# Attention on one Trainium2 core: scores, values and filler as three streams at uniform rates instead of units of two query tiles, with eight row buffers

## The chip, the cores and the metric

The kernel runs on one core of one Trainium2 chip, as one launch. The metric is the device time in microseconds (us). The kernel before was timed in three runs; the number compared is their median. A profiled execution of the same kernel was recorded beside them.

## The reference

One layer of a hybrid encoder on 1024 frames of width 1024: three token mixers beside each other, merged by sigmoid gates, then a gated MLP. What matters here are the two attentions, eight heads each, and the two other jobs that share the stage with them.

```python
hn = rms_norm(x, norm_mix_g[l])
u = hn @ w_in[l]
u_mla, u_fox, u_ssm, u_gate = jnp.split(u, split_at, axis=-1)
y_a = mla_branch(u_mla, ...) @ w_br_mla[l]
y_b = fox_branch(u_fox, ...) @ w_br_fox[l]
y_c = ssm_branch(u_ssm, ...) @ w_br_ssm[l]
g = jax.nn.sigmoid(u_gate + b_gate[l])
...
s = jnp.einsum('bqhd,bkhd->bhqk', q_blk, k).astype(jnp.float32) * scale
p = jax.nn.softmax(bias_mask(i, s), axis=-1).astype(v.dtype)
return jnp.einsum('bhqk,bkhd->bqhd', p, v)
```

MLA (the first eight heads) lets a query see all keys of its own and of earlier chunks of 64; FOX (the last eight) is causal with a decay. Both are computed row by row of 128 queries, and row i needs the keys of tiles 0 to i only.

## The kernel before

**The stage.** The kernel goes through input projections, the two attentions, the state-space scan (SSD), the merge of the branches, and the MLP. In the attention stage TensorE has three kinds of work, and the order in which it gets them is written out by hand: PE is under a manual schedule, and Python generators issue pieces of work in the order that a small planner chooses. The other engines get their instructions through a queue of due times.

**Scores** (`score_row`, L1288, through `scores`, L1332). For row i of a head, n = i + 1 key tiles: the score matmuls of one or two chunks of columns (at least 256 wide) into a PSUM buffer, three passes for an MLA head and two for a FOX head (`o.passes`). Then `finish` (L1310): for FOX one more matmul that adds the causal mask (L1313), and for both the softmax: row maximum on VectorE (L1314), exponential with row sum on ScalarE (L1316), reciprocal on VectorE and scaling on GpSimd (`norm`, L1319 to L1321). The row stands in one of the `a_pm` buffers (`Ring`, L1422), six of them. For FOX `finish` is put in the list `held`, so that the mask matmul can be placed right ahead of a group of transposes.

**Values** (`values`, L1337). For a unit jp, which is the two rows 2 jp and 2 jp + 1: transposes of the normalised rows in groups (L1379), split into a high and a low part by ScalarE (L1384) and VectorE (L1385), and the products with the values (`pv`, L1341), which run two key pairs behind the transposes (`PVLAG`, `pend`). Before its first transpose the function forces the softmax of both rows out of the queue (L1369). `done` (L1354) adds the two halves of the accumulator and stores them.

**Filler** (`all_fill`, L1163). 36 blocks of the remaining columns of the input projection (L1181), 12 with a convolution and 24 gates, in pieces of six matmuls. It is used to fill the waits of the attentions and of the SSD; whatever remains is issued after them.

**The planner.** Every generator yields the cost of what it has issued, in us of the planner's own clock `clk` (called plan-us below); `advance` (L1206) adds it to the clock, and `run_until` issues what has fallen due for the other engines. `merge` (L1222) takes a set of generators, each with its expected total, and always advances the one that has done the smallest part of its total, until all have ended.

**Units.** The loop at L1437 goes through 64 units (16 heads of four). In step n one `merge` runs together the scores of unit n, the values of unit n - 2, and filler of 1.08 times the cost of both (`FILL_ATT`, L1417; the share counts three passes for FOX too). A unit's values therefore start when the whole of the step after its scores has been issued. The costs are those of `cost_s` (L1411: columns times passes over 2400, and 0.1 per unit) and `cost_v` (L1414). With the score stream come the loads: at unit 0 of a head the queries and keys of the next head (`load_head`, L1257), at unit 3 its values (`load_values`, L1277, two buffers), all on the queue of SyncE, which also carries the filler's weights and all stores.

**After attention** the SSD stage (L1612) merges its own generators with filler of fixed amounts, and takes what filler there is.

The line that decides how far the values trail the scores:

```python
                if n >= 2:
                    share += cost_v(done[n - 2][1])
                    me = []
                    me.append(values(*done[n - 2], me))
                    tp_next[:] = me
                    st.append((me[0], cost_v(done[n - 2][1])))
                merge(st, FILL_ATT * share)
```

Of the kernel before, what the change touches and what calls it, by code (L numbers as in the profile page):

```python
# [11 lines left out]
F32 = mybir.dt.float32  # L12
# [9 lines left out]
P = 128  # L22
D = 1024
S = 1024
# [18 lines left out]
def block_kernel(ctx: ExitStack, tc: tile.TileContext, x, positions, norm_mix_g, w_in, b_gate,  # L43
# [581 lines left out]
    with ExitStack() as pm:  # L625
# [119 lines left out]
        def values():  # L745
            nonlocal step
            i = next(fxv)
            if i == NT:
                for _ in step:
                    pass  # L750
                vcols.append(v2)
            fox_values(i)
            next(step, None)
# [35 lines left out]
        units = 0  # L789
# [11 lines left out]
        for t in range(6):  # L801
# [4 lines left out]
            units = t  # L806
            fx_head.append(fx_bank())
            fx_part(fx_head[t], t, 0, 4, lambda k: w0[0][:, k, :], lambda k: w0[1][:, k, :])
        units = 0
# [25 lines left out]
    yv, yn, e, rec, s_, s2, q_, mn = (ft(n) for n in ("yv", "yn", "e", "rec", "s_", "s2", "q_", "mn"))  # L835
# [367 lines left out]
    fill = all_fill()  # L1203
    owed = [0.0]

    def advance(gen):  # L1206
        c = next(gen, None)
        if c is not None:
            clk[0] += c
            run_until(clk[0])  # L1210
        return c

    held, tp_next = [], []

    def flush():
        while held:
            held.pop(0)()
# [33 lines left out]
                s_[2] += c  # L1251


    class Head:
        pass

    def load_head(pool, br, h):  # L1257
        o = Head()
        o.br, o.h = br, h
        if (8 * br + h) % 2 == 0:  # L1260
            t = [e[:, i, :] for e in (w0p.tile([P, 2, S], F32R, name=uid(n), tag=n) for n in ("w0h", "w0l"))
                 for i in range(2)]
        else:
            t = [pool.tile([P, S], F32R, name=uid(n), tag=n, bufs=1) for n in ("qk0", "qk1", "qk2", "qk3")]
        if br == 0:
            parts = ((0, 0, k_h), (1, 0, k_l), (2, 0, q_h), (3, 0, q_l))
            kh, kl, qh, ql = (e[0:96] for e in t)
            o.passes = ((t[2][0:104], t[0][0:104]), (qh, kl), (ql, kh))
        else:
            parts = ((0, 0, fk_h), (1, 0, fk_h[:, 0:64, :]), (1, 64, fk_l), (2, 0, fq_h), (2, 64, fq_h), (3, 0, fq_l))  # L1270
            o.passes = ((t[2], t[1]), (t[3][0:68], t[0][0:68]))
        for i, r, src in parts:
            n = src.shape[1]
            SY.dma_start(f32(t[i][r:r + n, :]), src[h])
        return o

    def load_values(pool, o):  # L1277
        o.vv = pool.tile([P, NT, P], F32R, name=uid("vv"), tag="vv")
        SY.dma_start(f32(o.vv), (v_d, fv_d)[o.br].rearrange("(t p) h c -> p t h c", p=P)[:, :, o.h, :])
# [52 lines left out]
    def scores(o, jp, pn):  # L1332

        for i in (2 * jp, 2 * jp + 1):
            yield from score_row(o, i, pn)

    def values(o, jp, pn, me):  # L1337

        po = o_acc[:, jp % 2, :]

        def pv(kp, th, tl):  # L1341
            full = kp < jp
            k0, k1 = 2 * kp, 2 * kp + 1
            T.matmul(po, o.vv[:, k0, :], th[:, 0:256], start=kp == 0, stop=False)
            if full:
                T.matmul(po, o.vv[:, k1, :], th[:, 256:512], start=False, stop=False)
                T.matmul(po, o.vv[:, k1, :], tl[:, 256:512], start=False, stop=False)
            else:
                T.matmul(po[0:64, 128:256], o.vv[:, k1, 0:64], th[:, 256:384], start=False, stop=False)
                T.matmul(po[0:64, 128:256], o.vv[:, k1, 64:128], th[:, 256:384], start=False, stop=False)  # L1350
                T.matmul(po[0:64, 128:256], o.vv[:, k1, 0:64], tl[:, 256:384], start=False, stop=False)
            T.matmul(po, o.vv[:, k0, :], tl[:, 0:256], start=False, stop=not full)  # L1352

        def done():  # L1354
            o1, l1 = a_o1.get()
            o2, l2 = a_o2.get()
            later(0.5, lambda: A.activation(o1, po[64:128, :], AF.Copy))

            t_done[0] = clk[0]

            def fin():
                V.tensor_add(o2, po[0:64, :], o1)  # L1362
                SY.dma_start(att_d[o.br][o.h * 64:o.h * 64 + 64, jp * 256:jp * 256 + 256], o2)

            l1[0] = l2[0] = o_last[jp % 2] = later(0.9, fin)

        flush()
        for _, rl in pn:
            force(rl[0])  # L1369
        for k0 in range(0, jp + 1, 2):  # L1370
            flush()
            tp_next.clear()
            cs = 0.0
            for kp in range(k0, min(k0 + 2, jp + 1)):
                pt, pl = a_tp.get()
                off = 0
                for k in (2 * kp, 2 * kp + 1):
                    for qi in ((0, 1) if k <= 2 * jp else (1,)):
                        T.transpose(pt[:, off:off + P], pn[qi][0][:, k * P:k * P + P], ident)  # L1379
                        off += P  # L1380
                th, _ = a_th.get()
                tl, _ = a_tl.get()
                cs += 0.11 * off / P
                later(cs + 0.05, lambda th=th, pt=pt, off=off: A.activation(th[:, :off], pt[:, :off], AF.Copy))  # L1384
                pl[0] = later(cs + 0.6, lambda th=th, tl=tl, pt=pt, off=off: V.tensor_sub(  # L1385
                    tl[:, :off], pt[:, :off], f32(th[:, :off])))
                pend.append((pv, kp, th, tl, pl, jp, done if kp == jp else None))
            yield cs
            while len(pend) > PVLAG:
                if pend[0][1] == 0 and clk[0] - t_done[0] < 1.0:  # L1390
                    yield 0.0
                run_pv()
                if len(pend) <= PVLAG and k0 + 2 <= jp:
                    tp_next.append(me[0])
                yield 0.44

    PVLAG = 2
    pend = []
# [12 lines left out]
    def cost_s(jp, n=3):  # L1411
        return sum(n * max(b - a, 256) / 2400 for i in (2 * jp, 2 * jp + 1) for a, b in row_chunks(i)) + 0.1

    def cost_v(jp):  # L1414
        return 0.88 * jp + 0.33 + 0.39

    FILL_ATT = 1.08  # L1417
    FILL_SSD = [11.3] * 8 + [12.0, 24.5]
    with ExitStack() as pt__:
        atp = pt__.enter_context(TP("atp", 2))  # L1420
        psp = pt__.enter_context(TP("psa", 1, space=PSUM))
        a_pm = Ring(atp, [P, S], F32, "pm", 6)  # L1422
        a_nmx, a_rs = (Ring(atp, [P, 4], F32, n, 4) for n in ("nmx", "rs"))
        a_th, a_tl = (Ring(atp, [P, 512], F32R, n, PVLAG + 2) for n in ("pth", "ptl"))
        a_o1 = Ring(atp, [64, 256], F32, "o1", 1)
        a_o2 = Ring(atp, [64, 256], F32, "o2", 4)
        a_s = Ring(psp, [P, S], F32, "s", 2)
        a_tp = Ring(psp, [P, 512], F32, "tp", 2)
        o_acc = psp.tile([P, 2, 256], F32, name="o", tag="o")
        with tc.manual_schedule(engines={mybir.EngineType.PE}):  # L1430
            names = [(br, h) for br in range(2) for h in range(8)]
            merge([], 5.0)
            units = [(n, jp) for n in range(16) for jp in range(4)]
            heads = {0: load_head(atp, *names[0])}
            load_values(atp, heads[0])
            done = []
            for n in range(len(units) + 2):  # L1437
                st, share = [], 0.0
                if n < len(units):
                    hn_, jp = units[n]  # L1440
                    if jp == 0 and hn_ + 1 < 16:
                        heads[hn_ + 1] = load_head(atp, *names[hn_ + 1])
                    if jp == 3 and hn_ + 1 < 16:
                        load_values(atp, heads[hn_ + 1])
                    pn = []
                    done.append((heads[hn_], jp, pn))
                    share += cost_s(jp)
                    st.append((scores(heads[hn_], jp, pn), cost_s(jp, len(heads[hn_].passes))))
                if n >= 2:
                    share += cost_v(done[n - 2][1])  # L1450
                    me = []
                    me.append(values(*done[n - 2], me))
                    tp_next[:] = me
                    st.append((me[0], cost_v(done[n - 2][1])))
                merge(st, FILL_ATT * share)
            flush()
            while pend:
                run_pv()
                clk[0] += 0.44
                run_until(clk[0])  # L1460
            run_until(clk[0] + 3.0)
# [8 lines left out]
    with ExitStack() as ps__:  # L1470
# [141 lines left out]
        with tc.manual_schedule(engines={mybir.EngineType.PE}):  # L1612
# [6 lines left out]
            for c in range(NT + 2):  # L1619
                st = []  # L1620
# [13 lines left out]
    with ExitStack() as pe_:  # L1634
# [39 lines left out]
        for b, wsrc, nk in ((1, w_br_fox, 4), (0, w_br_mla, 4), (2, w_br_ssm, 8)):  # L1674
# [3 lines left out]
            for k in range(nk):  # L1678
# [13 lines left out]
                else:  # L1692
                    h, l = fox_hl[k] if b == 1 else ops_tile(4 + k)
                    e = split(h, l, raw)
# [8 lines left out]
            for j in range(NK):  # L1703
# [11 lines left out]
                g = fpl.tile([P, S], F32, name=uid("gl"), tag="t4", bufs=4)  # L1715
# [149 lines left out]
    for t, nh in units:  # L1865
        ns = slice(512 * nh, 512 * nh + 512)
        if nh == 0 and 4 <= t < 4 + FIRST:
            n = t - 4
# [341 lines left out]
```

## Time and profile before

| what | value |
|---|---|
| time, median of 3 runs | 2002.39 us (2002.23 to 2005.37) |
| profiled execution, its own time | 2000.52 us |
| profiled execution, first to last instruction | 1998.8 us |
| granted TensorE clock, mean | 1.000 |
| instructions | 28317 |
| attention stage, from the first filler matmuls to the last value products | 384.5 to 898.5 us |
| PE idle in that stage (514.0 us less 510.14 us busy) | 3.9 us |

Times in the profile count from the first instruction. PE is TensorE's matmuls, PEld its weight loads, DVE VectorE, ACT ScalarE, POOL GpSimd, SPq the transfer queue of SyncE. Rows of grouped instructions give count, busy time and the mean of one; rows in order of time give start and duration; an entry in square brackets is the engine's idle time ahead of the instruction and what ended it. A matmul's duration includes its way through the array, so consecutive matmuls overlap in the records, and what one costs PE is the distance from its start to the next one's.

### The profile page before, as it was taken

The page shows a single profiled execution, that of the slowest core. Times are in us where ns is not written, and L with a number is a line of the kernel's source. Part 1 is how long each engine was busy: PE and PEld are TensorE (multiplying, and loading weights), DVE is VectorE, ACT ScalarE, POOL GpSimd, SP SyncE. Part 2 cuts the span into 40 slices and gives each one's busy share as a digit, 9 for nine tenths or more (in the row PEclk, how much of TensorE's full clock was granted, in tenths as well). Part 3 has the DMA queues.
Part 4 walks back from the last instruction along what each step waited for, and adds up shares of the span by engine and source line. Part 5 has one row for each costly group of instructions (what it writes and reads, how often), then busy time and mean ns, then how long its engine had stood idle before and what let it go on. Part 6 is the DMA issues. An engine that isn't in the chain of part 4 may idle for free.

```text
span 1998.8 us, 28317 instructions
## 1 busy us (share of the span) xinstructions
PE 1975.3 (99%) x10185; PEld 1678.4 (84%) x10185; DVE 1340.1 (67%) x2153; ACT 929.3 (46%) x1650; POOL 660.1 (33%) x636
## 2 busy tenths in 40 slices
PE   8999999999999999999999999999999999999999
PEld 7989888888888888888888788888878888888887
DVE  7777567266656666656885476568998777665655
ACT  5555323255555555547775132225454445444432
POOL 5133322022222223213331262100664544523665
PEclk9999999999999999999999999999999999999999
DMA  5166857543535445427654786433332211249575
GB/s 179 52 195 211 276 178 226 166 126 105 139 114 146 116 124 134 127 78 238 182 193 137 258 278 211 139 125 104 107 95 85 76 61 49 79 154 336 195 259 193
DMA packets 278262, 312.15 MB, mean 156 GB/s; under 512 B 19197, under 2 KB 209289, under 8 KB 278122
## 3 DMA queue, kind: packets, MB, share of 16 engines
q1 hardware_dynamic: 278120, 310.35, 49.7%
q8 instruction: 80, 1.31, 0.3%
q14 instruction: 60, 0.49, 0.1%
q10 hardware_dynamic: 2, 0.00, 0.0%
HBM read 217.17 MB, written 93.13 MB: 155 GB/s over the span
## 4 chain that ended last, share of the span: by engine, by line
PE 88%; DVE 4%; DMA 3%; issue 2%; ACT 1%; POOL 1%; SPq 1%; ACTq 0%; DVEq 0%; POOLq 0%
PE mm L1181 18%; PE dn L2157 10%; PE fx L798 9%; PE ybr L1725 7%; PE ua L1816 6%; PE uc L1816 5%; PE ud L1816 4%; PE wo L1861 4%; PE s L1303 4%; PE tp L1379 3%; PE ub L1816 2%; PE fxv L188 2%; PE py L1570 1%; PE o L1352 1%; PE ckv L517 1%
## 5 line engine op out<-in xcount | busy, mean ns | idle before, releaser
L1321 POOL TENSOR_SCALAR pm<-pm,rs 128x128 f32<-128x128 f32 (+7 forms) x128 | 115.8, 906 | 403.0 <-DVE rs L1320 378.7
L1181 PE MATMUL mm<-hnh,wh 128*128 128x512 f32 x576 | 237.9, 413 | 0.0
L1181 PE MATMUL mm<-hnh,wl 128*128 128x512 f32 x576 | 225.9, 392 | 0.0
L1181 PE MATMUL mm<-hnl,wh 128*128 128x512 f32 x576 | 225.6, 392 | 0.0
L2157 PE MATMUL dn<-dr,dr 128*128 128x512 f32 x592 | 182.3, 389 | 0.0
L1385 DVE TENSOR_TENSOR ptl<-tp,pth 128x512 fp32r<-128x512 f32 (+1 forms) x160 | 98.7, 631 | 70.5 <-ACT pth L1384 69.9
L2157 PEld LDWEIGHTS dn<-dr,dr 128*128 128x128 f32 x592 | 111.1, 188 | 23.0
L1384 ACT ACTIVATE pth<-tp 128x512 fp32r<-128x512 f32 (+1 forms) x160 | 85.4, 555 | 94.5 <-PE tp L1379 94.3
L1181 PEld LDWEIGHTS mm<-hnh,wl 128*128 128x128 f32 x576 | 108.2, 188 | 24.8
L1316 ACT ACTIVATE pm<-s,nmx 128x128 f32<-128x128 f32 (+7 forms) x128 | 94.6, 741 | 71.8 <-DVE nmx L1314 71.3
L1314 DVE TENSOR_REDUCE nmx<-s 128x1 f32<-128x128 f32 (+7 forms) x128 | 95.3, 751 | 48.8 <-PE s L1303 26.9
L1181 PEld LDWEIGHTS mm<-hnl,wh 128*128 128x128 f32 x576 | 108.8, 189 | 15.9
L1181 PEld LDWEIGHTS mm<-hnh,wh 128*128 128x128 f32 x576 | 108.7, 189 | 16.1 <-DVE o L1362 0.2
L2157 PE MATMUL dn<-dr 128*128 128x512 f32 x296 | 115.2, 389 | 0.0
L135 DVE TENSOR_TENSOR dr<-dr,dr 128x1024 fp32r<-128x1024 f32 x52 | 71.5, 1382 | 52.1 <-ACT dr L134 48.1
L1725 PE MATMUL ybr<-ah,wl 128*128 128x512 f32 x256 | 99.7, 389 | 0.7 <-DVE wl L135 0.7
L1725 PE MATMUL ybr<-ah,wh 128*128 128x512 f32 x256 | 99.7, 389 | 0.3 <-ACT wh L134 0.3
L1725 PE MATMUL ybr<-al,wh 128*128 128x512 f32 x256 | 99.8, 390 | 0.0
L134 ACT ACTIVATE dr<-dr 128x1024 fp32r<-128x1024 f32 x52 | 55.1, 1061 | 71.7 <-PE dn L2157 51.0
L134 ACT ACTIVATE wh<-wr 128x1024 fp32r<-128x1024 f32 (+1 forms) x40 | 35.1, 877 | 97.8 <-PE ybr L1725 44.3
L1379 PE MATMUL tp<-ident,pm 128*128 128x128 f32 x576 | 79.1, 273 | 0.0
L135 DVE TENSOR_TENSOR wl<-S,wh 128x1024 fp32r<-128x1024 f32 x42 | 63.1, 1503 | 23.3 <-ACT wh L134 23.3
(528 smaller groups left out, 5705.3 us busy)
## 6 DMA issues: line engine op xcount, KB each, us to landing
dr<-act_d SPq DMA_DIRECT2D x99, 256.0 KB
wr<-in_w_in_dram SPq DMA_DIRECT2D x36, 512.0 KB
g_d<-t SPq DMA_DIRECT2D x24, 512.0 KB
gl<-g_d SPq DMA_DIRECT2D x24, 512.0 KB
wr<-in_ffn_w_up_dram SPq DMA_DIRECT2D x23, 512.0 KB
ws<-in_ffn_w_down_dram SPq DMA_DIRECT2D x22, 512.0 KB
wsum_d<-ws SPq DMA_DIRECT2D x22, 512.0 KB
act_d<-fa SPq DMA_DIRECT2D x22, 512.0 KB
```

Of the source, the lines that this page charges most:

```text
L134: i = A.activation(h, src, AF.Copy) if he is A else he.tensor_copy(h, src)
L135: return i, le.tensor_sub(l, src, f32(h))
L798: T.matmul(p, a(k), b(k), start=k == 0 and i == 0, stop=k == NK - 1 and i == 2)
L1181: T.matmul(ps, a[:, k, :], b[half][:, k, :], start=(k == 0 and i == 0), stop=(k == NK - 1 and i == 2))
L1314: later(t0 + 0.15, lambda: V.reduce_max(nmx[:, 0:1], row, axis=AX, negate=True))
L1316: pl[0] = later(t1, lambda: A.activation(p_[:, 0:n * P], row, AF.Exp, bias=nmx[:, 0:1], accum_out=rs[:, 0:1]))
L1321: G.tensor_scalar(p_[:, 0:n * P], p_[:, 0:n * P], rs[:, 1:2], 0.0, op0=ALU.mult, op1=ALU.add)
L1379: T.transpose(pt[:, off:off + P], pn[qi][0][:, k * P:k * P + P], ident)
L1385: pl[0] = later(cs + 0.6, lambda th=th, tl=tl, pt=pt, off=off: V.tensor_sub(tl[:, :off], pt[:, :off], f32(th[:, :off])))
L1725: T.matmul(pss[half], w_[:, k, :], a_[k][:, hs], start=k == 0 and i == 0, stop=k == nk - 1 and i == 2)
L1816: T.matmul(ps, a, b, start=first and n == 0, stop=n == 11, skip_group_check=not first)
L2157: T.matmul(ps[m], a[:, ts_], b[:, 512:], start=first_ and j == 0 and q == 0, stop=j == NFH - 1 and q == 2, skip_group_check=not first_)
```

## The change

The loop over units and its `merge` are replaced by one call of a new function `weave` with three endless streams: all scores of the 16 heads, all values, and the filler. Each stream has a counter of progress, in heads, that grows by the issued cost divided by the stream's cost per head; the stream with the smallest counter goes next. Scores start at 0, values at `LAG` = 0.62, filler at -0.6. The cost per head of the filler is 13.0 plan-us while the values are in the MLA heads and 15.4 after that. If a stream has nothing to issue (it yields 0.0), the next one goes. A unit's values wait, without issuing anything, until both of its rows have their score matmuls issued. Two further edits: the values stream is offered for pairing with a held mask after every group of products, also across units, and at most two pending products; and there are eight row buffers instead of six.

```diff
+    def weave(streams):
+
+        st = [[g, lead, per] for g, lead, per in streams]
+        while any(e[0] is not fill for e in st):
+            s_ = min(st, key=lambda e: e[1])
+            if held:
+                v = [e for e in st if e[0] in tp_next]
+                if v and v[0][1] <= s_[1] + 0.04:
+                    s_ = v[0]
+                else:
+                    flush()
+            c = advance(s_[0])
+            if c == 0.0:
+                rest = [e for e in st if e is not s_]
+                if rest:
+                    s_ = min(rest, key=lambda e: e[1])
+                    c = advance(s_[0])
+            if c is None:
+                st.remove(s_)
+            else:
+                s_[1] += c / s_[2]()
...
+            if len(pend) <= PVLAG:
+                tp_next.append(me[0])
             yield cs
...
-                if len(pend) <= PVLAG and k0 + 2 <= jp:
+                if len(pend) <= PVLAG:
                     tp_next.append(me[0])
...
-    FILL_ATT = 1.08
+    FILL_HEAD = (13.0, 15.4)
+    LAG = 0.62
...
-        a_pm = Ring(atp, [P, S], F32, "pm", 6)
+        a_pm = Ring(atp, [P, S], F32, "pm", 8)
...
-            units = [(n, jp) for n in range(16) for jp in range(4)]
...
-            for n in range(len(units) + 2):
...
-                merge(st, FILL_ATT * share)
+            todo = []
+            at = [0, 0]
+
+            def all_scores():
+                for n in range(16):
+                    at[0] = n // 8
+                    for jp in range(4):
+                        if jp == 0 and n + 1 < 16:
+                            heads[n + 1] = load_head(atp, *names[n + 1])
+                        if jp == 3 and n + 1 < 16:
+                            load_values(atp, heads[n + 1])
+                        pn = []
+                        todo.append((heads[n], jp, pn))
+                        yield from scores(heads[n], jp, pn)
+
+            me = []
+
+            def all_values():
+                for n in range(64):
+                    at[1] = n // 32
+                    while n >= len(todo) or len(todo[n][2]) < 2:
+                        yield 0.0
+                    yield from values(*todo[n], me)
+
+            me.append(all_values())
+            tp_next[:] = me
+            scores_ = lambda: sum(cost_s(jp, 3 - at[0]) - 0.1 for jp in range(4))
+            values_ = lambda: sum(cost_v(jp) for jp in range(4))
+            weave([(all_scores(), 0.0, scores_), (me[0], LAG, values_), (fill, -0.6, lambda: FILL_HEAD[at[1]])])
```

More of the change, by code (lines that the diff above doesn't have):

```diff
@@ L1432, in block_kernel @@
             merge([], 5.0)
-            units = [(n, jp) for n in range(16) for jp in range(4)]
             heads = {0: load_head(atp, *names[0])}
             load_values(atp, heads[0])
-            done = []
-            for n in range(len(units) + 2):
[L1438 to L1454, printed above, removed]
-                merge(st, FILL_ATT * share)
+            todo = []
[23 more added lines that the diff above has]
+            weave([(all_scores(), 0.0, scores_), (me[0], LAG, values_), (fill, -0.6, lambda: FILL_HEAD[at[1]])])
             flush()
```

## The prediction

> **What bounds the kernel now.** The page comes first: span, busy shares, the row of PE over the span, the clock that was granted, and the chain that ended last.
>
> ```profile
> span 1998.8 us, 28317 instructions
> ...
> PE 1975.3 (99%) x10185; PEld 1678.4 (84%) x10185; DVE 1340.1 (67%) x2153; ACT 929.3 (46%) x1650; POOL 660.1 (33%) x636
> ...
> PE   8999999999999999999999999999999999999999
> ...
> PEclk9999999999999999999999999999999999999999
> ...
> PE 88%; DVE 4%; DMA 3%; issue 2%; ACT 1%; POOL 1%; SPq 1%; ACTq 0%; DVEq 0%; POOLq 0%
> PE mm L1181 18%; PE dn L2157 10%; PE fx L798 9%; PE ybr L1725 7%; PE ua L1816 6%; PE uc L1816 5%; PE ud L1816 4%; PE wo L1861 4%; PE s L1303 4%; PE tp L1379 3%; PE ub L1816 2%; PE fxv L188 2%; PE py L1570 1%; PE o L1352 1%; PE ckv L517 1%
> ```
>
> PE is busy for 1975.3 of 1998.8 us, at a full clock, and the chain lies on it for 88%. A change in the order of its work can take away its waits or add some; it can't shorten the work. So I look next at the stage that is changed, and at what follows it, by windows (length, then busy time and count of PE, PEld, DVE, ACT, POOL, then clock, share and rate of the transfers), and at PE's waits in the stage.
>
> ```profile
> 384.50:641.90 257.40, 254.58 (x1485) 222.74 (x1485) 154.54 (x298) 132.05 (x286) 64.43 (x72) 1.00 0.47 126
> 641.90:898.50 256.60, 255.56 (x1539) 217.56 (x1539) 162.11 (x302) 137.38 (x292) 65.49 (x68) 1.00 0.43 121
> 898.50:1092.80 194.30, 189.98 (x1050) 161.92 (x1048) 139.52 (x186) 135.61 (x283) 57.28 (x79) 1.00 0.59 185
> ```
>
> ```profile
> PE o L1344 <- DVE o L1362: 3.1, 3, 2.3
> PE s L1303 <- ACT pm L1316: 0.5, 1, 0.5
> PE o L1344 <- ACT o L1357: 0.2, 1, 0.2
> ```
>
> In the two halves of the attention stage (MLA heads, FOX heads) PE is idle for 257.4 - 254.58 = 2.8 and 256.6 - 255.56 = 1.0 us. The waits that are named come to 3.8 us, nearly all for the accumulator that the VectorE has not emptied yet. DVE and ACT are busy for 54 to 63% and POOL for 25%, so no other engine is near its limit. All that a better order can win here is 3.9 us, and it must not bring new waits. The margin that keeps them away shows in head 13 (heads count from 0, FOX has 8 to 15), in order of time:
>
> ```profile
> 817.37 0.62 PE L1303 MATMUL s<-qk,qk 128*128 128x512 f32 x2
> ...
> 817.83 0.23 PE L1313 MATMUL s<-mfox,identb 128*128 128x128 bf16 x1
> ...
> 817.87 0.36 PE L1344 MATMUL o<-pth,vv 128*128 128x256 f32 x1
> ...
> 818.07 0.22 PE L1349 MATMUL o<-pth,vv 128*64 128x128 f32 x1
> ...
> 818.09 1.42 DVE L1314 TENSOR_REDUCE nmx<-s 128x1 f32<-128x1024 f32 x2 [0.85 <-PE s L1313]
> ...
> 818.65 0.23 PE L1313 MATMUL s<-mfox,identb 128*128 128x128 bf16 x1
> ...
> 818.72 1.04 PE L1379 MATMUL tp<-ident,pm 128*128 128x128 f32 x8
> ...
> 819.37 0.60 ACT L1384 ACTIVATE pth<-tp 128x512 fp32r<-128x512 f32 x1 [0.37 <-PE tp L1379]
> ...
> 820.00 0.69 DVE L1385 TENSOR_TENSOR ptl<-tp,pth 128x512 fp32r<-128x512 f32 x1 [0.16 <-ACT pth L1384]
> ...
> 820.20 1.12 ACT L1316 ACTIVATE pm<-s,nmx 128x1024 f32<-128x1024 f32 x1
> ...
> 820.99 0.28 PE L1344 MATMUL o<-pth,vv 128*128 128x256 f32 x1
> ...
> 821.11 0.28 PE L1346 MATMUL o<-pth,vv 128*128 128x256 f32 x1
> ...
> 821.20 0.21 ACT L1316 ACTIVATION_READ_ACCUMULATOR pm<-s,nmx 128x1 f32 x1
> ...
> 821.44 0.16 DVE L1320 RECIPROCAL rs<-rs 128x1 f32<-128x1 f32 x1 [0.69 <-ACT pm L1316]
> ...
> 821.77 1.12 POOL L1321 TENSOR_SCALAR pm<-pm,rs 128x1024 f32<-128x1024 f32 x1 [0.48 <-DVE rs L1320]
> ...
> 826.27 1.04 PE L1379 MATMUL tp<-ident,pm 128*128 128x128 f32 x8
> ```
>
> The last scores of row 7 end with their mask matmul at 817.83 + 0.23 = 818.06. Then the row goes through maximum (its 1.22 of the 1.42 for two), exponential 1.12, sum 0.21, reciprocal 0.16 and scaling 1.12; the scaled row is there at 821.77 + 1.12 = 822.89, a chain of 4.8 us, of which 3.8 are durations. The transposes that read it start at 826.27, 8.2 us after the scores: a reserve of 3.4 us. The chain is not always that short; in head 8 other work lies between, and the same row (the second of the two in this POOL row) is ready 671.60 - 664.16 = 7.4 us after its mask:
>
> ```profile
> 663.93 0.23 PE L1313 MATMUL s<-mfox,identb 128*128 128x128 bf16 x1
> ```
>
> ```profile
> 669.38 2.22 POOL L1321 TENSOR_SCALAR pm<-pm,rs 128x128 f32<-128x128 f32 x2 [4.33 <-PE tp L1379]
> ```
>
> **The change part by part.** Removed: nothing that PE computes. All score matmuls, transposes, products and 36 filler blocks remain; what moves is their order. So the sum is one of waits.
>
> *How far the values trail.* In the units the trail can't shrink, since a whole step lies between. In `weave` it follows from the three counters, which can be worked out from the code's numbers. A head's rows have 4736 score columns. An MLA head yields 4736 x 3 / 2400 = 5.92 plan-us and is divided by 5.92: 1.000 progress per head. A FOX head yields 4736 x 2 / 2400 = 3.947 plus 0.05 in each of its 8 rows, 4.347 in all, but `scores_` takes the 0.1 per unit off again and divides by 3.947: 1.1014 per head. A head of values yields 36 transposes at 0.11 and 10 products at 0.44, 8.36, divided by 8.16: 1.0245 per head. So in the MLA heads the values fall back from 0.605 heads to 0.80, and in the FOX heads the scores lose 0.077 progress per head against the values, eight times: the trail shrinks to 0.2 heads. That is the point on which I forecast.
>
> *From progress to us.* A FOX head before takes 28.35 plan-us (filler 1.08 x 14.48 = 15.64, scores 4.35, values 8.36). Four of them lie between this row and the transposes of 826.27 above:
>
> ```profile
> 703.45 0.72 PE L1379 MATMUL tp<-ident,pm 128*128 128x128 f32 x5
> ```
>
> (826.27 - 703.45) / 4 = 30.7 us, 1.083 us per plan-us. After the change one unit of progress has 3.947 + 8.16 + 15.4 = 27.5 plan-us, 29.8 us of PE work.
>
> *The gaps.* The counter grows when a piece is issued, so the last chunk of row 7 of FOX head j (0 to 7) is issued when the least counter is 8 + 1.1014 (j + 1) - 0.121 = 8.981 + 1.1014 j, and the transposes of unit 3 (0.592 of a head's values lie before it) at 0.62 + 1.0245 (8.592 + j) = 9.423 + 1.0245 j. The difference, times 29.8 and less 0.5 us for the chunk itself (0.46 us and the mask of the rows above), is 12.7 - 2.29 j us. For unit 2 the same working gives 15.6 - 2.29 j, for unit 1 19.9 - 2.29 j (3.9 at the last, enough for its short rows). Against them stand the chains: 4.8 us for row 7; for row 5 the rows of the FOX heads
>
> ```profile
> L1320 DVE RECIPROCAL rs<-rs 128x1 f32<-128x1 f32 x62 | 9.8, 158 | 19.4 <-ACT pm L1316 19.4
> ...
> L1314 DVE TENSOR_REDUCE nmx<-s 128x1 f32<-128x768 f32 x8 | 7.7, 957 | 2.2 <-PE s L1313 1.9
> L1321 POOL TENSOR_SCALAR pm<-pm,rs 128x768 f32<-128x768 f32 x8 | 7.6, 952 | 16.4 <-DVE rs L1320 16.4
> ...
> L1316 ACT ACTIVATE pm<-s,nmx 128x768 f32<-128x768 f32 x8 | 7.2, 900 | 0.0
> ```
>
> give 0.96 + 0.90 + 0.16 + 0.95 and the sum's 0.2 = 3.2, with handovers 3.8. What the gap lacks, PE waits, because its order is fixed and everything behind the transposes (filler too) stands behind them:
>
> | FOX head j | unit 3 gap, wait | unit 2 gap, wait |
> |---|---|---|
> | 3 | 5.8, 0 | 8.7, 0 |
> | 4 | 3.5, 1.3 | 6.4, 0 |
> | 5 | 1.3, 3.5 | 4.2, 0 |
> | 6 | below 0, 4.8 | 1.9, 1.9 |
> | 7 | below 0, 4.8 | below 0, 3.8 |
>
> Below 0 the values yield 0.0 until the scores are out and then come directly behind them, so the whole chain is paid. Sum: 14.4 + 5.7 = 20.1 us. MLA heads: the same formula gives 9 us for head 0 and more later, against chains of about 5: nothing. Bounds: with chains of 4.3 and 3.3 and gaps longer by 1.5 us (half a piece of work: a filler step is 1.3 plan-us of 27.5 and makes the order grainy) 12 us; with chains of 5.7 and 4.2 and gaps shorter by 1.5, 34 us. I take the 4.8, the chain of the undisturbed head, because a waiting PE also starves the filler's work that lengthened the other.
>
> *The seams.* The waits for the accumulator go where two units' products met at the end of a step; in one stream a group of transposes lies between. Gain between 0 and 3.9 us, the whole idle time; I take 3.9, as nothing else puts these products together.
>
> *Pairing.* There are 64 mask matmuls:
>
> ```profile
> L1313 PE MATMUL s<-mfox,identb x64: 230/231/233, 634.3 to 878.9; 128*128 128x128 bf16 x64
> ```
>
> A mask ahead of transposes costs 818.72 - 818.65 = 0.07 us; ahead of a product 0.04 and 0.08 more in the product behind it (818.07 - 817.87 = 0.20 to the next start, where 821.11 - 820.99 = 0.12 is usual). The wider offer may save 0.05 on each: 0 to 3.2 us, I take 1.0.
>
> *The end.* After the last scores only values are left, and the last two products wait for the split of the last transposes, where filler covered that before. By the rows of head 13 that is 0.60 for ACT and twice 0.69 for DVE less two products of four matmuls, 0.12 each: 1.0 us. Bounds 0 (the filler's last piece falls there) and 2.0 (it covers nothing).
>
> *Row buffers.* Eight suffice as long as the trail is under 0.889 heads (row 6 of the next head must not come before the old row 6 is transposed, at 0.895 of the values' head); it reaches 0.80. Six would have stopped at 0.54. Cost 0: eight rows of 4 KB a partition, no instruction more.
>
> *Loads.* `load_head` and `load_values` stay at the same units of the scores, but the value buffer of two heads back is now free later: its last products run some 0.2 to 0.35 progress after the load is called for, 6 to 10 us. SyncE's queue waits there already:
>
> ```profile
> SPq L1279 <- PE o L1352: 115.1, 14, 15.1
> ```
>
> 8.2 us in the mean, 15.1 at the longest, and none of PE's three waits is for a transfer; the values are wanted 0.87 progress (25 us) after the call. Behind it stand the filler's weights, the next head's queries and keys and the stores; the weights are called for a block ahead, 10.4 plan-us of filler or some 20 us. Cost 0; if that cover failed, up to 5 us in the MLA half.
>
> *Filler.* Attention uses 13.0 x 9.42 + 15.4 x 8.09 = 247 plan-us instead of 16 x 15.64 = 250; the 3 that remain are done in the SSD stage. Work that PE does elsewhere: 0.
>
> Sum: 20.1 - 3.9 - 1.0 + 1.0 = +16.2 us. The profiled execution took 2000.52 us (span 1998.8 and 1.7 around it), so 2016.7 there; the median of the runs is 1.87 us above it, so 2018.6 for the median.
>
> *The clock.* PE's longest idle time in the stage now, at 535.4, left the clock where it was:
>
> ```profile
> 535.00:538.10 3.10, 0.80 (x5) 0.33 (x3) 2.30 (x4) 0.71 (x2) 0.70 (x1) 1.00 0.84 201
> ```
>
> Its 2.3 us of waiting show a clock of 1.00. The Trainium skill ("TensorE: Matmul & The Clock Gate", section "Why this matters for your kernels") advises against idle gaps of PE over about 3 us, after which the clock falls back to half. No wait here is that long, so the trace neither bears it out nor refutes it. By that rule four of the new waits would each cost some work at half speed too, some 2027 us as an estimate. The forecast goes without it.
>
> **The rivals.** *Faster:* the waits don't come (gaps longer by more than I allow, or chains near their 3.8 us of pure durations), and the seams and the pairing are won: 2002.4 - 3.9 - 2.0 = 1996.5 us. For it: the chains are 3.8 us of work, and the gap of the first heads is wider than now (12.7 against 8.2 us). Against: a trail of 0.2 heads is shorter than unit 3 itself, so that the last two heads must wait whatever the chain is. It decides where all waits together stay under 2 us.
>
> *No change:* the grain falls well, only the two last heads wait, some 6 us, against 5 won: 2002 to 2006.
>
> *Half clock:* after a wait of over 2.3 us, the longest seen, PE runs at half speed for as long as it has waited. Four waits of the table are longer (3.5, 4.8, 4.8, 3.8); they come to 16.9 us, half of which is lost again: 2018.6 + 8.5 = 2027 us. Nothing in this trace is for it but that no longer wait was tried.
>
> *The change does not do what it says:* streams that drift, or are blocked, are not uniform. That is the forecast itself, in the FOX half.
>
> **How the numbers follow.** A measurement tells about 0.2% (4 us) from no change. Forecast, slower by the waits of the late FOX heads: 0.60, with its own range from 2002.4 + 12 - 3.9 - 2 = 2008.5 to 2002.4 + 34 + 2.0 - 2 = 2036. Half clock: 0.08. Faster: 0.20. No change: 0.12. Slower in all 0.68. The range from 1997 to 2034 takes in no change, the slower case but for its upper end, and a quarter of the faster case; left out are 0.15 of that and some 0.04 above.
>
> **What would show it.** In the profile after: PE's waits list transposes (L1379) behind the scaling on GpSimd (L1321), some 20 us, none before 740 us and most in the last three FOX heads, the longest near 4.8 us; the waits on L1362 gone; PE idle in the FOX half about 20 us and in the MLA half under 2; the SSD stage as long as before plus some 3 us; later stages unchanged. If transposes don't wait, the working of the trail is wrong; if they wait already in the MLA heads, the start value 0.62 is too small for the chain; if the clock row shows less than 1.00, the rival of the half clock holds.

## The result, and the profile after

The changed kernel takes 2056.4 us (median of 4 runs, 2055.1 to 2058.7), the kernel before 2002.3 us on the same chip: 1.0268 times as long, 95% interval 1.0251 to 1.0286. The forecast was 2018.6 us with a range up to 2034. Slower was right and so was the reason; the size was not.

The page of the changed kernel: span, busy time, the row of PE over the span, the granted clock, the chain.

```profile
span 2053.4 us, 28322 instructions
...
PE 1995.7 (97%) x10185; PEld 1691.2 (82%) x10185; DVE 1343.7 (65%) x2153; ACT 934.0 (45%) x1650; POOL 655.8 (32%) x636
...
PE   9999999999999989778999999999999999999999
...
PEclk9999999999999999889999999999999999999999
...
PE 85%; DVE 6%; issue 3%; ACT 3%; POOL 2%; DMA 1%; SPq 0%; ACTq 0%; POOLq 0%; DVEq 0%
```

The same matmuls are now busy for 1995.7 instead of 1975.3 us, four slices of PE (the 8, 7, 7 and 8 in the middle) fall under nine tenths, and the clock row, all nines before, has two eights there. So two things went wrong in one place: PE waits, and it works more slowly. The windows (MLA heads, FOX heads, SSD; columns as in the prediction) say where, and PE's waits in attention (total, times, longest) say for what.

```profile
388.80:629.70 240.90, 237.30 (x1396) 207.96 (x1394) 149.15 (x282) 128.23 (x273) 60.37 (x70) 1.00 0.45 125
629.70:947.20 317.50, 280.82 (x1578) 235.20 (x1577) 170.83 (x317) 145.52 (x303) 61.63 (x71) 0.95 0.37 102
947.20:1147.80 200.60, 196.00 (x1074) 166.60 (x1074) 141.31 (x186) 135.80 (x283) 60.29 (x79) 1.00 0.56 180
```

```profile
PE tp L1402 <- POOL pm L1344: 32.4, 13, 4.5
PE o L1367 <- DVE o L1385: 3.9, 7, 1.3
PE o L1367 <- ACT o L1380: 1.6, 3, 1.0
```

The FOX half has 36.7 us without work on PE and a mean clock of 0.95. Attention as a whole, from the first score to the last product, against the same stretch before (the first block is the changed kernel; the second is the kernel before, attention and then SSD):

```profile
388.80:947.20 558.40, 518.12 (x2972) 443.16 (x2971) 319.98 (x599) 273.75 (x575) 121.99 (x140) 0.97 0.41 112
```

```profile
390.00:898.40 508.40, 504.55 (x2997) 435.73 (x2996) 315.96 (x599) 268.78 (x576) 129.92 (x140) 1.00 0.45 123
898.40:1092.60 194.20, 189.88 (x1051) 161.97 (x1049) 139.32 (x185) 135.64 (x282) 57.28 (x79) 1.00 0.59 185
```

Attention grew by 50.0 us: idle time by (558.40 - 518.12) - (508.40 - 504.55) = 36.4, busy time by 13.6, although 25 filler matmuls fewer lie in it (2972 matmuls against 2997; the other kinds are the same). Those 25, some 0.23 us each or 5.7 in all, went to the SSD, which grew by 200.6 - 194.2 = 6.4 us. What lies before and after is 1.8 us shorter.

One of the waits, and what it brings, in order of time (head 14, unit 3, in the changed kernel):

```profile
884.77 0.23 PE L1336 MATMUL s<-mfox,identb 128*128 128x128 bf16 x1
...
884.83 0.28 PE L1402 MATMUL tp<-ident,pm 128*128 128x128 f32 x1
885.03 1.23 DVE L1337 TENSOR_REDUCE nmx<-s 128x1 f32<-128x1024 f32 x1 [3.56 <-PE s L1336]
...
886.35 1.12 ACT L1339 ACTIVATE pm<-s,nmx 128x1024 f32<-128x1024 f32 x1 [4.13 <-DVE nmx L1337]
...
887.85 1.12 POOL L1344 TENSOR_SCALAR pm<-pm,rs 128x1024 f32<-128x1024 f32 x1 [5.27 <-DVE rs L1343]
...
889.02 1.16 PE L1402 MATMUL tp<-ident,pm 128*128 128x128 f32 x7 [3.91 <-POOL pm L1344]
...
891.69 0.63 PE L1181 MATMUL mm<-hnh,wh 128*128 128x512 f32 x1
...
892.11 0.63 PE L1181 MATMUL mm<-hnl,wh 128*128 128x512 f32 x1
...
892.97 0.47 PE L1181 MATMUL mm<-hnh,wh 128*128 128x512 f32 x1
...
893.27 0.40 PE L1181 MATMUL mm<-hnl,wh 128*128 128x512 f32 x1
893.50 0.39 PE L1181 MATMUL mm<-hnh,wl 128*128 128x512 f32 x1
```

The transposes follow the mask of their own row at once. The first reads row 6 and runs; the second needs row 7 and stands for 3.91 us while DVE, ACT, DVE and POOL, all idle until then, take their turns. After that the filler's matmuls start 892.11 - 891.69 = 0.42 us apart, from 893.27 on 0.23. The windows over that stretch and over the first such one show the clock:

```profile
763.40:770.23 6.83, 6.10 (x20) 5.13 (x21) 1.84 (x4) 2.00 (x5) 0.73 (x2) 0.50 0.65 140
...
889.70:893.11 3.41, 3.41 (x16) 3.12 (x15) 1.78 (x3) 1.48 (x3) 0.00 (x0) 0.50 0.30 89
```

There are seven such stretches, 34.1 us with 31.3 us of PE work in them. At full speed that work takes half, so about 15.7 us are lost.

### The profile page after: what moved, and what is told of

It is laid out like the page before. It is cut to its first block, busy times and chain, and to the rows that moved or that the text cites. A ratio compares the mean times of both kernels' runs of the same rounds, so it can differ in the third digit from the quotient of the medians.

```text
span 2053.4 us, 28322 instructions
## 1 busy us (share of the span) xinstructions
PE 1995.7 (97%) x10185; PEld 1691.2 (82%) x10185; DVE 1343.7 (65%) x2153; ACT 934.0 (45%) x1650; POOL 655.8 (32%) x636
## 4 chain that ended last, share of the span: by engine, by line
PE 85%; DVE 6%; issue 3%; ACT 3%; POOL 2%; DMA 1%; SPq 0%; ACTq 0%; POOLq 0%; DVEq 0%
PE mm L1181 16%; PE dn L2191 10%; PE fx L798 9%; PE ybr L1759 9%; PE ua L1850 5%; PE uc L1850 5%; PE ud L1850 4%; PE wo L1895 4%; PE s L1326 4%; PE tp L1402 3%; PE ub L1850 2%; PE fxv L188 2%; PE o L1367 1%; PE ckv L517 1%; PE cq L517 1%
## 5 line engine op out<-in xcount | busy, mean ns | idle before, releaser
L1344 POOL TENSOR_SCALAR pm<-pm,rs 128x128 f32<-128x128 f32 (+7 forms) x128 | 107.7, 843 | 445.1 <-DVE rs L1343 427.2
L1402 PE MATMUL tp<-ident,pm 128*128 128x128 f32 x576 | 85.3, 282 | 33.8 <-POOL pm L1344 32.4
L1402 PEld LDWEIGHTS tp<-ident,pm 128*128 128x128 f32 x576 | 68.6, 144 | 42.3 <-POOL pm L1344 35.7
```

Source lines behind the costliest of these rows:

```text
L1344: G.tensor_scalar(p_[:, 0:n * P], p_[:, 0:n * P], rs[:, 1:2], 0.0, op0=ALU.mult, op1=ALU.add)
```

## The experiments

The theory after the result: the score rate that is too small for the FOX heads makes the values catch up (the waits for GpSimd), the waits cost twice because PE's clock falls to half behind them, and the rest is small. The rivals: the streams as such are dear, the eight buffers are, or the waits carry everything and the clock nothing. Times are medians; each is set against runs of the kernel before on its own chip: 2000.6 us for the first four, 1999.8 for the next four, 2001.3 for the last. By that measure the changed kernel is +54.1.

**1. The score rate made true.**

```
-            scores_ = lambda: sum(cost_s(jp, 3 - at[0]) - 0.1 for jp in range(4))
+            scores_ = lambda: sum(cost_s(jp, 3 - at[0]) - 0.1 * (1 - at[0]) for jp in range(4))
```

> The changed kernel with one number put right: the progress of a FOX head of scores is counted with its 0.05 per row (4.347 plan-us per head and not 3.947), so that scores and values run at 1.000 and 1.0245 progress per head all through. Theory (the trail of the values shrinks in the FOX heads because the scores are counted too fast): the trail grows from 0.5 to 0.9 heads, no group of transposes waits for the scaling on GpSimd after the first heads, the clock stays at 1.00, and the time is 2000 to 2008 us. Rival (uniform streams as such bring the waits, by the order in which the other engines get their work, whatever the rates): most of the waits stay, 2040 us or more.

2013.7 us, 1.0065 times the kernel before (1.005 to 1.008): +13.1. The waits for GpSimd are gone; row 7's gap, from its last score to unit 3's first transpose, is 10.7 to 17.2 us in the FOX heads. PE's longest waits now (two rows), and its attention and SSD:

```profile
PE o L1367 <- DVE o L1385: 4.7, 9, 1.1
PE o L1367 <- ACT o L1380: 3.3, 5, 1.4
```

```profile
388.00:902.30 514.30, 503.34 (x2975) 431.97 (x2974) 317.83 (x598) 272.33 (x575) 121.51 (x140) 1.00 0.45 121
902.30:1104.40 202.10, 195.38 (x1071) 165.97 (x1070) 140.25 (x187) 135.33 (x283) 60.47 (x79) 1.00 0.57 181
```

One constant carries 41 of the 54 us; that settles the main cause. But the 2000 to 2008 us that I expected were missed: the waits for the output bank are 8.0 us, not less than the 3.3 of before.

**2. More lead for the values:** `LAG = 0.80` instead of 0.62, the rate left wrong.

> The changed kernel with the start of the values at 0.80 in place of 0.62, the drift left in. Theory: every gap is 0.18 x 29.8 = 5.4 us longer; the transposes of unit 3 begin to wait at head 12 or 13 and not at head 10, some 15 us of waits in all in place of 32, two or three stretches of half clock in place of seven, 2015 to 2035 us. Rival (the rates and the start do not decide): 2056 us as before. In the MLA heads the trail nears 0.88, where eight row buffers just suffice; if they do not, the exponential of row 6 waits there for the old transposes.

2022.5 us, 1.0111 (1.0094 to 1.0128).

```profile
PE tp L1402 <- POOL pm L1344: 9.7, 3, 4.2
```

The waits stay, later and fewer, as the drift would have it. By the prediction's own formula 0.18 more lead (5.4 us) leaves only 0.5 + 2.8 = 3.3 us of waits; 9.7 came, with two stretches at half clock behind them. So the formula's gaps are too long; more on that below.

**3. Eight row buffers alone:** the kernel before with 8 instead of 6.

> The kernel before, in units, with eight row buffers alone. Both theories: no row waits for a buffer before, so no change, 2002.3 us within 2. A rival that lays part of the loss on the larger buffers (memory shifted, transfers later) expects some us more.

2001.8 us, 1.0003 (0.9994 to 1.0012): no difference. Its trace holds a stretch at half clock that the kernel before doesn't have, behind the same wait of 2.3 us (the trace of experiment 11 has one there too):

```profile
536.57:539.98 3.41, 3.41 (x18) 3.31 (x17) 1.63 (x5) 2.06 (x6) 0.38 (x1) 0.50 0.99 225
```

**4. Waits put into the kernel before,** growing, about 70 us apart: scalings by 1.0 on GpSimd ahead of row 7's own, in every second head.

```
                 V.reciprocal(rs[:, 1:2], rs[:, 0:1])
+                if n == 8 and o.h % 2 == 1:
+                    for _ in range(4 + 4 * o.br + o.h // 2):
+                        G.tensor_scalar(p_[:, 0:n * P], p_[:, 0:n * P], 1.0, 0.0, op0=ALU.mult, op1=ALU.add)
```

> A probe of the clock on the kernel before: in every second head the scaled row 7 is multiplied by 1.0 again, 4, 5, 6 and 7 times in MLA heads 1, 3, 5, 7 and 8 to 11 times in FOX heads 9, 11, 13, 15, 1.12 us each. The reserve of 3.4 us takes up the first three, so PE waits once per such head for about 1, 2, 3.5, 4.5, 5.5, 6.5, 8 and 9 us, some 40 us in all. Theory (an idle time longer than some bound between 2.3 and 4 us brings half clock for whole windows of about 3.4 us): no half clock after the first two, half clock after the last four, 2045 to 2060 us. Rival (half clock follows from the sum of many waits close together, not from one long wait): none here, since the waits lie 60 us apart, and about 2042 us.

2071.8 us, one run. The waits came to 54.5 us, where I had expected some 40, and the time lies above the expected range. Here they are, and the stretch at half clock at the longest one, most of the wait included:

```profile
PE tp L1382 <- POOL pm L1324: 54.5, 8, 10.1
```

```profile
876.00:889.60 13.60, 6.08 (x18) 5.12 (x19) 3.75 (x5) 2.03 (x3) 7.04 (x8) 0.50 0.10 30
```

Each of the eight waits, the first of 3.67 us included, brought half clock, 71.7 us of it in all with the one stretch behind the wait of 2.3 us for the output bank. I had expected none after the first two: the point from which it sets in is lower than I took it to be, and lone waits suffice.

**5. The same waits, filled with empty work.** Matmuls of the values with themselves go into the transposes' buffer ahead of ten units and are overwritten there; 113 in all, each row of them shorter than the wait that it fills.

```
                 pt, pl = a_tp.get()
+                if kp == 0:
+                    for _ in range(EMPTY.get((8 * o.br + o.h, jp), 0)):
+                        T.matmul(pt, o.vv[:, 0, :], o.vv[:, 0:4, :], start=True, stop=True)
...
+    EMPTY = {(11, 3): 14, (12, 3): 9, (13, 3): 15, (14, 1): 8, (14, 2): 12, (14, 3): 15,
+             (15, 1): 9, (15, 2): 18, (15, 3): 9, (10, 3): 4}
```

> The changed kernel with empty matmuls on TensorE (a product of the values with themselves into the transposes' buffer, overwritten by the transposes) ahead of the ten units of heads 10 to 15 that wait longest for GpSimd, each row of them some 0.3 us shorter than the wait it stands in; order, streams and rates are untouched. If the half-speed stretches (34.1 us in the changed kernel's trace, so some 17 us lost) come from TensorE standing idle in those waits, they go and the time falls by 12 to 17 us, to 2039 to 2045 us, with the granted clock near 1.0, though the waited time (32 us) is still there as empty work. The rival, that the waits alone carry the loss and the half speed costs nothing beside them: 2055 to 2059 us, as the changed kernel.

2044.3 us, 1.0224 (1.0207 to 1.0241): +44.6, so 9.5 us less than the changed kernel by the two differences and 12.1 by the medians. Its waits and its attention:

```profile
PE tp L1405 <- POOL pm L1344: 6.3, 12, 1.8
```

```profile
388.10:932.70 544.60, 530.06 (x3085) 451.14 (x3085) 319.34 (x599) 273.28 (x575) 123.19 (x140) 1.00 0.42 115
```

The time that is lost to GpSimd is still there: 113 x 0.229 = 25.9 us of empty work and 6.3 of waits, 32.2 against 32.4. The half clock is gone, and PE's own work in attention takes 530.1 - 25.9 = 504.2 instead of 518.1 us. So the clock costs 13.9 us of work in attention by the traces and 9.5 to 12.1 us by the times, which also hold what differs elsewhere. That it costs this is shown by taking it away with the order and the lost time kept.

**6. Filler back into attention:** experiment 1 with `FILL_HEAD = (13.35, 15.8)`.

> The first experiment (score rate true in the FOX heads, 2013.7 us) with the filler's shares raised by 2.7%, to 13.35 and 15.8, so that attention uses up as many filler matmuls as the kernel before (31 more, 7.1 us). If the filler is only moved between two stages that TensorE bounds, attention grows by 7 us, the SSD shrinks by 7, and the time stays at 2012 to 2015 us. The rival, that the filler left over is dear in the SSD or missing as cover in attention: 2004 to 2009 us.

2012.5 us, 1.0059 (1.0044 to 1.0074), the same as experiment 1 within the intervals. 26 matmuls came back (counted to the last product), and the SSD shrank from 202.1 to 195.5 us. Moved filler is neutral here.

**7. The seams.** Experiment 1 with a longer hold on a unit's first product, which takes over the output bank.

```
-                if pend[0][1] == 0 and clk[0] - t_done[0] < 1.0:
-                    yield 0.0
+                for _ in range(6):
+                    if pend[0][1] == 0 and clk[0] - t_done[0] < 2.2:
+                        yield 0.0
```

> The first experiment with the hold on a unit's first product (which takes the output bank that the unit two earlier has just left) raised from 1.0 to 2.2 us of the plan's clock, with up to six turns of the other streams instead of one. If the 8 us of waits on the output bank (o, from VectorE and ScalarE) are what is left of attention's loss, they fall to under 3 us and the time to 2006 to 2010 us. The rival, that the bank's waits turn into others (the transposes' buffer, the split of the transposes), leaves 2012 to 2016 us.

2006.4 us, 1.0032 (1.002 to 1.0044): +6.6, so 6.5 us less than experiment 1. The waits for the output bank fall from 8.0 to 0.6 us; of others, only the filler's matmuls wait more for ACT (2.0 us instead of 0.8).

```profile
388.10:895.60 507.50, 502.84 (x2975) 432.70 (x2974) 317.84 (x598) 272.24 (x575) 121.96 (x140) 1.00 0.46 122
895.60:1095.70 200.10, 195.19 (x1072) 166.08 (x1071) 142.62 (x187) 135.74 (x283) 60.45 (x79) 1.00 0.57 183
```

**8. Six row buffers in the changed kernel.**

> The changed kernel with six row buffers in place of eight. If the buffers carry nothing at this order, as the prediction had it, 2054 to 2060 us and the same waits. The rival, that a values stream 0.5 to 0.7 heads behind holds more than six rows: scores and their exponentials wait for a buffer, at 5 us or more in the first eight heads and at their end, 2062 us or more.

2058.8 us, 1.0295 (1.028 to 1.0311), which overlaps the changed kernel's interval; the waits for GpSimd are 32.7 us and those of the scores for a buffer 1.0 us, as with eight. Two buffers fewer cost nothing at this order, and the prediction's "six would have stopped at 0.54" is wrong.

**9. Rate, seams and filler together.**

> Three steps in one: the score rate true in the FOX heads, the hold on a unit's first product at 2.2 us with up to six turns, and the filler's shares raised by 2.7% (13.35 and 15.8). If the three terms found so far (waits for GpSimd with the half speed, waits on the output bank, filler put off to the SSD) are all that separates the two kernels: 1998 to 2003 us beside some 2000 of the kernel before. The rival, that the finer mix of the streams itself costs TensorE time (6 us more in attention after the waits are taken out, in the last experiment's trace): 2004 to 2008 us.

2007.8 us, 1.0034 (1.0022 to 1.0047): +6.5, in the rival's range. Attention, with hardly a wait left:

```profile
388.00:899.50 511.50, 507.65 (x3001) 437.19 (x2999) 319.01 (x599) 273.54 (x577) 123.59 (x140) 1.00 0.47 122
```

PE's busy time is 3.1 us above that of the kernel before, with four filler matmuls more (0.9 us); experiments 1, 5 and 7 give 3 to 5 us in the same way once their missing filler is added (502.8 + 5.0, 504.2 + 5.7 against 504.6). So a finer mix of the streams goes with some 2 to 5 us more of busy time. That the mix is the cause isn't shown; which neighbours cost it wasn't tried.

**10. Less filler in the attention of the kernel before:** `FILL_ATT = 1.052` instead of 1.08.

> The kernel before with its attention's filler share lowered from 1.08 to 1.052, which puts about 31 filler matmuls (7 us) off to the SSD; nothing else is changed. If filler is only moved between two stages that TensorE bounds, attention shrinks by about 7 us, the SSD grows by about 7 and the time is that of the kernel before within 2 us. The rival, that late filler is dear: 3 to 7 us more than the kernel before.

2009.6 us, 1.0046 (1.0033 to 1.0058): dear, by 8.3 us.

```profile
390.00:891.30 501.30, 497.16 (x2953) 427.27 (x2951) 316.92 (x597) 269.85 (x575) 122.77 (x140) 1.00 0.45 123
891.30:1103.00 211.70, 204.56 (x1094) 173.90 (x1094) 144.42 (x190) 136.99 (x285) 63.58 (x79) 0.98 0.56 176
```

44 matmuls moved (10.1 us, more than meant). In this execution (2012.5 us, above the median) attention won 7.1 us and the SSD lost 17.5: the 10.1, three stretches at half clock (10.2 us, some 5 lost) and 2.8 more idle. Together with experiment 6 this speaks for late filler being dear only where PE then waits long enough for its clock to fall; a run with those waits filled, which would show it, wasn't made.

**11. The seams of the kernel before:** the hold of experiment 7 there.

> The kernel before with the hold on a unit's first product raised from 1.0 to 2.2 us of the plan's clock and up to six turns of the other stream. Its waits on the output bank are 3.9 us in its trace; if they go without others in their place, 2 to 4 us faster (1996 to 1998 us beside some 2000). The rival, that the values' products are put off at the end of a unit, where nothing else is left to do, and wait just the same: within 1 us of the kernel before.

2000.8 us, 0.9998 (0.9989 to 1.0007): nothing, and its trace has the same three waits for the output bank on DVE (3.1 us). The rival's figure was right; its reason, that at the end of a step there is nothing else to put in, fits but wasn't traced.

**12. Both rates true.** Experiment 9 with `cost_v(jp) + 0.05` in `values_` and `LAG = 0.8`.

> The combined kernel (true score rate, 2.2 us hold with six turns, filler shares 13.35 and 15.8) with the values' rate counted at what it yields as well (8.36 a head in place of 8.16) and the values' lead at 0.80 heads, so that the values stay as far behind as they start. If the gap need only be longer than the chain, nothing is gained over the combined kernel: within 2 us of it. The rival, that the values drifting to some 0.9 heads behind leave too much for the end of attention and too little to mix: 3 to 6 us faster than the combined kernel.

2005.4 us, 1.0022 (1.0013 to 1.0031): 2.4 us less than experiment 9 on the same chip. The intervals overlap, but five of the six runs of experiment 9 lie above all eleven of this one, so the difference is probably real; it falls between what I expected (within 2) and the rival (3 to 6). By the traces it isn't in the streams: from the first score to the end of the SSD experiment 12 takes 708.3 us and experiment 9 708.7, and the rest lies behind the SSD (906.5 against 909.3 us), where experiment 9 has a stretch at half clock (at 1097.74) and experiment 12 none. So nothing shows a gain from more or less gap once it exceeds the chain. No version of the streams beat the kernel before.

## Why the prediction was wrong, point by point

**Right: the trail.** The prediction divided what a FOX head of scores yields (4.347) by what `scores_` counts (3.947) and had the values catch up from 0.8 to 0.2 heads. Experiment 1 changes only this and takes away every wait for GpSimd. The sign, the engine, the line and the place in the last heads were as forecast.

**Wrong, the step that failed first: the gaps (12.7 - 2.29 j and its two companions).** The working put a unit's transposes where all earlier products of the values have been counted. But two products always stay pending (`PVLAG`), and their 0.88 plan-us are never paid ahead: the values run 0.88 / 8.16 = 0.108 progress, 3.2 us, further ahead than the formula has them. In the trace the gap of row 7 in FOX heads 0, 1, 2 is 9.2, 5.5 and 2.9 us where the formula gave 12.7, 10.4 and 8.1. Of these 3.5, 4.9 and 5.2 us the pending products account for 3.2, as worked out from the code (no run changes `PVLAG`); the cause of the rest stays open. Here is head 2 (head 10 of the 16): the end of row 7's scores and mask, and the transposes.

```profile
724.03 0.23 PE L1336 MATMUL s<-mfox,identb 128*128 128x128 bf16 x1
...
727.18 0.27 PE L1402 MATMUL tp<-ident,pm 128*128 128x128 f32 x1
728.69 0.98 PE L1402 MATMUL tp<-ident,pm 128*128 128x128 f32 x7 [1.23 <-POOL pm L1344]
```

So the waits began two heads early, and unit 1, which was to have enough, waited too. With 3.2 us taken off each gap and chains of 4.0, 3.3 and 2.6 us (the shortest that came out for rows 7, 5 and 3), the same working gives 28 us for the changed kernel and 9 for experiment 2; 32.4 and 9.7 were measured.

| FOX head j | predicted waits (units 3, 2, 1) | measured |
|---|---|---|
| 2 | 0, 0, 0 | 1.2, 0, 0 |
| 3 | 0, 0, 0 | 3.5, 0, 0 |
| 4 | 1.3, 0, 0 | 2.5, 0.8, 0 |
| 5 | 3.5, 0, 0 | 3.9, 0.4, 0 |
| 6 | 4.8, 1.9, 0 | 3.9, 3.2, 2.2 |
| 7 | 4.8, 3.8, 0 | 3.7, 4.5, 2.5 |
| sum | 20.1 | 32.4 |

**Wrong, the second step: "The forecast goes without it" (the half clock).** It was a rival at 0.08 and 8.5 us; experiment 5 measures 13.9 us of work in attention. The one row it was judged by, 2.3 us of waiting at a clock of 1.00, was too little to judge by: in experiment 3 the same wait did bring half clock. The rule of the Trainium skill ("TensorE: Matmul & The Clock Gate", "Why this matters for your kernels"), no idle gaps of over about 3 us, would have led the right way. The traces agree with it: of the waits of 3 us or more in the 14 traces, between 380 and 1160 us, 22 of 23 brought half clock; some shorter ones did too, as the last section shows.

**Wrong, the third: the seams (-3.9) and the pairing (-1.0).** Waits for the output bank rose from 3.3 to 5.5 us, and to 8.0 in experiment 1. "A group of transposes lies between" is true, but three transposes are 0.5 us, and the bank's emptying queues on ACT, behind an exponential in two of the ten waits of the changed kernel (748.78 and 831.58) and behind the filler's own activations in others (685.96, 716.46, 878.72). Experiment 7 prices the seams of experiment 1 at 6.5 us. Of 64 masks 18 stand directly ahead of transposes, where it was 24: the pairing was lost rather than won. It wasn't priced alone, but experiment 12, where no mask stands there, is no slower than experiment 9 with 13.

**Smaller terms.** Buffers at 0 and loads at 0 were right: none of PE's waits in attention is for a transfer. Filler at 0 was near (+6.4 us in the SSD for 5.7 taken from attention). The chain of 4.8 was too long for the waiting heads (4.0), since the engines are idle when they are needed; that hid a part of the error in the gaps.

The miss adds up: waits 32.4 instead of 20.1 (+12.3), the clock 13.9 instead of 0, seams and pairing +2.2 instead of -4.9 (+7.1, taking their waits alone), the finer mix 2 to 5. That is 35 to 38 us, as against 2056.4 - 2018.6 = 37.8; with the 9.5 to 12.1 us that the times of experiment 5 give for the clock it is 31 to 36. The range failed because it joined long waits with no half clock, although by these traces half clock comes with waits of the length that its 34 us are made of. (By the chains and gaps that the prediction names for that bound, units 3 and 2 come to 22.1 + 9.6 = 31.7 us; what unit 1 adds it doesn't say.) What stays open is the cause of the 4 to 7 us that the mended streams (experiments 7, 9, 12) take above the kernel before. By their traces it lies between the first score and the end of the SSD: 707.6, 708.7 and 708.3 us against 702.6.

## What to carry to other kernels

Where counters decide the order of a queue that can't be reordered later, work out what each stream really yields against what it is divided by, over the whole stage and with everything that stays pending: 10% in one rate used up the reserve within three heads. Price a long wait of TensorE at its length and half of the work in the slow stretch behind it, and let terms with one cause move together in the range. Here a gap longer than the chain brought nothing that the traces show.

## What the hardware showed unexpectedly

The stretches at half clock are all 3.41 us long or a multiple of it, and within a trace their starts lie on one grid of 3.41 us (763.40, 841.91 and 858.98 in the changed kernel are 23 and 5 steps apart). I laid PE's idle times over 0.1 us (380 to 1160 us) onto that grid in the ten traces that show it: behind all 43 steps with 1.75 us or more of idle time, the next step ran at half clock. With less, a step at full speed was followed by half clock twice (1.27 and 1.66 us idle), and by full speed in every other case, up to 1.71 us; 0.7 to 1.7 us could prolong a slow stretch. So a wait of 2.2 us counts if it falls into one step (2.17 us, ended at 857.73: half clock from 858.98) and a longer one doesn't if it is cut in two (2.53 us, ended at 904.86: none). The Trainium skill ("TensorE: Matmul & The Clock Gate", "Part 1: The HAM clock gate") has a monitor with a free-running window of about 3.4 us; the grid agrees with that.
